# A row softmax: another split of the first loads, and a wait ahead of the third

## The chip, the cores and the metric

The kernel runs on one core of a Trainium2 chip. The metric is the device time of one execution in microseconds. Profile times count from the first instruction of the profiled execution (the start of its span). VectorE, ScalarE, GpSimd and SyncE stand in the profile as DVE, ACT, POOL and SP; a "q" behind an engine's name marks work of its instruction queue, such as the issue of a DMA. TensorE has no work here.

## The reference

The input x is float32 of 16 x 1024 x 512. Softmax is taken over the last axis:

```python
x_max = np.max(x, axis=-1, keepdims=True)
exp_x = np.exp(x - x_max)
return exp_x / np.sum(exp_x, axis=-1, keepdims=True)
```

That makes 16,384 rows of 512 elements (2 KB each). 33.55 MB are read and 33.55 MB are written.

## The kernel before

The 16,384 rows lie on 128 partitions, 128 rows to each. `CHUNKS` (line 13) cuts these 128 into ten chunks: the first number is the rows per partition, the second the place in the tile `held`, which has room for 96 rows per partition. The chunks have 3, 5, 8 and then seven times 16 rows. One load brings a chunk, all its rows of a partition as one contiguous piece: 6, 10, 16 or 32 KB per partition. In the text, load 1 is that of the first chunk, load 2 that of the second, and so on to load 10 (in the code they have the indices 0 to 9).

All work is in place in `held`. A chunk is worked on in groups of about 8 rows (`GROUP`; a chunk of 16 rows makes two groups). For each group there are three steps:

- `rowmax` (line 98): one VectorE reduction over the whole group, at line 101, which gives the negated maxima.
- `exps` (line 105): for each row one ScalarE exponential with the maximum as bias, which also gives the row's sum (line 109).
- `scale` (line 118): one VectorE reciprocal (line 121) and for each row one VectorE multiplication (line 123); then the store of the finished rows is issued on ScalarE's queue (line 129).

The order is written out by hand (line 136 and after). SyncE issues the loads, all at line 96. Indices 0 to 7 (`EARLY`) are issued ahead of everything else, and `loads_at_the_head` (line 33) puts the very first before the barrier at the program's start. The loads with the indices 8 and 9 go into places that earlier chunks have left; they are issued after the chunks with the indices 2 and 3 (`AFTER_STORE`) and wait for the stores of those rows. Each engine works in program order. The group loop takes the maxima and exponentials of a group before the scaling of the group ahead of it, except at the start of chunks with the indices 1, 2 and 3 (`FINISH_BEFORE`), where the earlier group is finished first. Each DMA counts up a semaphore when it lands. There are eight of these, and they are used again, so that some loads wait for an earlier DMA before they are issued: the sixth waits for the first, the seventh for the second and the eighth for the fourth.

Chunks with the indices 3, 4 and 5 are stored in two halves (`STORE_ROWS`), the others whole. That makes 13 stores.

Of the kernel before, what the change touches and what calls it, by code (L numbers as in the profile page):

```python
# [1 line left out]

# [4 lines left out]

F32 = mybir.dt.float32
EXP = mybir.ActivationFunctionType.Exp
AX = mybir.AxisListType.X  # L10


CHUNKS = [
    (3, 0), (5, 3), (8, 8), (16, 16), (16, 32), (16, 48), (16, 64), (16, 80), (16, 0), (16, 16),
]
SBUF_ROWS = 96

EARLY = 8
AFTER_STORE = {2: [8], 3: [9]}

GROUP = 8

FINISH_BEFORE = (1, 2, 3)

STORE_ROWS = {3: 8, 4: 8, 5: 8}

ON_ACT = ()

AT_HEAD = {mybir.EngineType.SP: 1}

def loads_at_the_head(nc):

    main, body = nc.main_func.blocks[0], nc.main_func.blocks[1]
    for engine, count in AT_HEAD.items():
        loads = [
            i
            for i in body.instructions
            if i.engine == engine and type(i).__name__ == "InstDMACopy"  # L40
        ][:count]
        barrier = next(
            n
            for n, i in enumerate(main.instructions)
            if i.engine == engine and type(i).__name__ == "InstDrain"
        )
        for load in loads:
            body.instructions.remove(load)
        main.instructions[barrier:barrier] = loads


@with_exitstack
def kernel(
    ctx: ExitStack,
    tc: tile.TileContext,
    x: bass.AP,
    out: bass.AP,
):
    nc = tc.nc
    nc.at_finalize(loads_at_the_head)  # L60
    P = nc.NUM_PARTITIONS

    x_flat = x.flatten_outer_dims()
    out_flat = out.flatten_outer_dims()
    n, d = x_flat.shape
    assert n == P * sum(R for R, _ in CHUNKS)


    src, dst, at = [], [], 0
    for R, _ in CHUNKS:  # L70
        for flat, views in ((x_flat, src), (out_flat, dst)):
            part = flat[at : at + P * R, :]
            views.append(part.rearrange("(p r) d -> p r d", r=R))
        at += P * R

    data = ctx.enter_context(tc.tile_pool(name="data", bufs=1))
    stats = ctx.enter_context(tc.tile_pool(name="stats", bufs=4))
    held = data.tile([P, SBUF_ROWS, d], F32, name="held")
    place = [held[:, s : s + R, :] for R, s in CHUNKS]


    groups = []
    for k, (R, _) in enumerate(CHUNKS):
        m = max(1, round(R / GROUP))
        cuts = [R * i // m for i in range(m + 1)]
        since = 0
        for a, b in zip(cuts, cuts[1:]):
            ends = b == R or b - since >= STORE_ROWS.get(k, R)
            groups.append((k, a, b, since if ends else None))
            since = b if ends else since  # L90
    shift = [None] * len(groups)
    sums = [None] * len(groups)

    def load(k):
        queue = nc.scalar if k in ON_ACT else nc.sync
        queue.dma_start(out=place[k], in_=src[k])

    def rowmax(g):
        k, a, b, _ = groups[g]
        shift[g] = stats.tile([P, b - a], F32, name="shift", tag="shift")  # L100
        nc.vector.reduce_max(  # L101
            out=shift[g], in_=place[k][:, a:b, :], axis=AX, negate=True
        )

    def exps(g):
        k, a, b, _ = groups[g]
        sums[g] = stats.tile([P, b - a], F32, name="sums", tag="sums")
        for r in range(a, b):
            nc.scalar.activation(  # L109
                out=place[k][:, r, :],  # L110
                in_=place[k][:, r, :],
                func=EXP,
                bias=shift[g][:, r - a : r - a + 1],
                scale=1.0,
                accum_out=sums[g][:, r - a : r - a + 1],
            )

    def scale(g):
        k, a, b, since = groups[g]
        recip = stats.tile([P, b - a], F32, name="recip", tag="recip")  # L120
        nc.vector.reciprocal(out=recip, in_=sums[g])  # L121
        for r in range(a, b):
            nc.vector.tensor_scalar_mul(  # L123
                out=place[k][:, r, :],
                in0=place[k][:, r, :],
                scalar1=recip[:, r - a : r - a + 1],
            )
        if since is not None:
            nc.scalar.dma_start(
                out=dst[k][:, since:b, :], in_=place[k][:, since:b, :]  # L130
            )
        if b == CHUNKS[k][0]:
            for later in AFTER_STORE.get(k, ()):
                load(later)

    with tc.manual_schedule():
        for k in range(EARLY):
            load(k)
        waiting = None
        for g, (k, a, _, _) in enumerate(groups):  # L140
            if waiting is not None and a == 0 and k in FINISH_BEFORE:
                scale(waiting)
                waiting = None
            rowmax(g)
            exps(g)
            if waiting is not None:
                scale(waiting)
            waiting = g
        scale(waiting)


# [1 line left out]
_INS = ['x']  # L153
_OUTS = [((16, 1024, 512), 'float32')]


# [23 lines left out]
```

## Time and profile before

| what | us |
|---|---|
| median of four runs | 161.55 |
| lowest, highest | 161.53, 161.78 |
| the profiled execution | 161.78 |
| its span, first to last instruction | 160.0 |
| VectorE busy | 123.9 |
| ScalarE busy | 93.3 |
| first load, issue to landing | 4.4 |
| second load (5 rows), issue to landing | 7.8 |
| third load (8 rows), issue to landing | 12.3 |
| last store issued at | 144.77 |

The profiled execution is the slowest of the four. What its time has beyond the span, 1.78 us, lies before the first and after the last instruction.

The busy time of an engine is the sum over its instructions, without issues of DMAs and waits. DMA is the mean busy share of sixteen DMA engines. Queue q1 holds the loads, q10 the stores. The trace also records each packet: here a packet is one partition's piece of a load or a store, and each of the sixteen DMA engines carries eight pieces of every load, and then a 4-byte mark that counts up the semaphore. GB/s of a window counts the packets that start in it.

### The profile page before, as it was taken

To read this page: it belongs to the slowest core of one execution; us is meant where nothing else is said; L and a number is where in the kernel's file an instruction comes from. 1 tells how busy PE (TensorE), PEld (TensorE's weight loads), DVE (VectorE), ACT (ScalarE), POOL (GpSimd) and SP (SyncE) were. 2 spreads that over 40 slices of the span, in tenths; PEclk is the share of its full clock that TensorE was granted. 3 is DMA by queue.
4 is the path that set the end of the run, shared out by engine and by line. 5 is a ranking of instruction groups with operands and counts; after the bars stand their busy time and mean duration, and the time that the engine had idled before them with its cause. 6 is when DMAs were issued, how large, how long until landed. Compare 5 with 4: busy or idle time off the path is not lost.

```text
span 160.0 us, 521 instructions
## 1 busy us (share of the span) xinstructions
DVE 123.9 (77%) x162; ACT 93.3 (58%) x257; POOL 0.2 (0%) x4
## 2 busy tenths in 40 slices
DVE  0481870799699999999999999999999999661000
ACT  0718029208994959595867777685959595930000
POOL 0000000000000000000000000000000000000000
DMA  7999999999999999999999999999999999999993
GB/s 253 374 475 373 446 456 416 417 426 452 406 428 438 483 410 399 434 442 467 406 414 434 442 463 418 399 442 418 442 447 451 410 434 467 401 426 475 410 426 164
DMA packets 3315, 67.13 MB, mean 420 GB/s; under 512 B 368, under 2 KB 368, under 8 KB 624
## 3 DMA queue, kind: packets, MB, share of 16 engines
q1 hardware_dynamic: 1440, 33.56, 49.5%
q10 hardware_dynamic: 1872, 33.56, 48.8%
q14 instruction: 3, 0.02, 0.0%
HBM read 33.55 MB, written 33.55 MB: 419 GB/s over the span
## 4 chain that ended last, share of the span: by engine, by line
DVE 70%; ACT 14%; issue 3%; DMA 3%; DVEq 0%; ACTq 0%
DVE shift L101 38%; DVE held L123 30%; ACT held L109 14%; DMA held<-in_x_dram 3%; DVE recip L121 2%; DVEq L175 0%; ACTq L109 0%
## 5 line engine op out<-in xcount | busy, mean ns | idle before, releaser
L109 ACT ACTIVATE held<-held,shift 128x512 f32<-128x512 f32 x128 | 90.5, 709 | 43.4 <-DVE shift L101 33.3
L101 DVE TENSOR_REDUCE shift<-held 128x8 f32<-128x4096 f32 (+2 forms) x17 | 70.7, 4162 | 4.5 <-DMA held<-in_x_dram 4.5
L123 DVE TENSOR_SCALAR held<-held,recip 128x512 f32<-128x512 f32 x128 | 52.2, 482 | 0.6
L109 ACT ACTIVATION_READ_ACCUMULATOR held<-held,shift 128x1 f32 x128 | 23.9, 187 | 0.0
L121 DVE RECIPROCAL recip<-sums 128x8 f32<-128x8 f32 (+2 forms) x17 | 3.3, 194 | 15.8 <-ACT held L109 15.8
L109 ACT ACT_TABLE_LOAD x1 | 1.3, 1283 | 4.5 <-DMA held<-in_x_dram 4.5
L164 POOL MEMSET const-bfloat16-1.0<- 128x1 bf16 x1 | 0.1, 102 | 0.0
L164 POOL MEMSET const-uint8-127<- 128x1 uint8 x1 | 0.1, 102 | 0.0
L164 POOL MEMSET const-float32-1.0<- 128x1 f32 x1 | 0.1, 99 | 0.0
L164 POOL MEMSET const-float32-0.0<- 128x1 f32 x1 | 0.1, 98 | 0.2 <-issue 0.2
## 6 DMA issues: line engine op xcount, KB each, us to landing
held<-in_x_dram SPq DMA_DIRECT2D x7, 4096.0 KB, 43.0
out_dram<-held ACTq DMA_DIRECT2D x4, 4096.0 KB, 21.3
out_dram<-held ACTq DMA_DIRECT2D x7, 2048.0 KB, 35.7
held<-in_x_dram SPq DMA_DIRECT2D x1, 2048.0 KB, 12.3
held<-in_x_dram SPq DMA_DIRECT2D x1, 1280.0 KB, 7.8
out_dram<-held ACTq DMA_DIRECT2D x1, 1280.0 KB, 19.5
held<-in_x_dram SPq DMA_DIRECT2D x1, 768.0 KB, 4.4
out_dram<-held ACTq DMA_DIRECT2D x1, 768.0 KB, 15.4
```

The source lines that it names most:

```text
L101: nc.vector.reduce_max(out=shift[g], in_=place[k][:, a:b, :], axis=AX, negate=True)
L109: nc.scalar.activation(out=place[k][:, r, :], in_=place[k][:, r, :], func=EXP, bias=shift[g][:, r - a : r - a + 1], scale=1.0, accum_out=s ...
L121: nc.vector.reciprocal(out=recip, in_=sums[g])
L123: nc.vector.tensor_scalar_mul(out=place[k][:, r, :], in0=place[k][:, r, :], scalar1=recip[:, r - a : r - a + 1],)
L164: nc = _bacc.Bacc("TRN2", target_bir_lowering=False, num_devices=1)
```

## The change

Two things change. The second and third chunk change places in size: the first loads have 3, 8 and 5 rows per partition, and the places in `held` follow. And each load from the third on is made to depend on the first: it is issued once the first has landed.

```diff
 CHUNKS = [
-    (3, 0), (5, 3), (8, 8), (16, 16), (16, 32), (16, 48), (16, 64), (16, 80), (16, 0), (16, 16),
+    (3, 0), (8, 3), (5, 11), (16, 16), (16, 32), (16, 48), (16, 64), (16, 80), (16, 0), (16, 16),
 ]
...
+ONCE_LANDED = 2
...
+    queued = [None] * len(CHUNKS)
     shift = [None] * len(groups)
     sums = [None] * len(groups)
 
     def load(k):
         queue = nc.scalar if k in ON_ACT else nc.sync
-        queue.dma_start(out=place[k], in_=src[k])
+        queued[k] = queue.dma_start(out=place[k], in_=src[k])
+        if k >= ONCE_LANDED:
+            tc.add_manual_dep(
+                queued[k].ins,
+                queued[0].ins.name,
+                mybir.DependencyInfo(
+                    mybir.DependencyClass.Sync, mybir.DependencyReason.DATA
+                ),
+                reason="the first load gets the descriptor generator first",
+            )
```

The second load carries no such wait. `add_manual_dep` makes the instruction named first wait for the completion of the second.

## The prediction

> **What bounds the kernel now.** I read the page's slices and queues first, then DMA rates by stretch, then the timelines of SP and VectorE, and last the packet records of the trace. The page, parts 2 and 3 (40 slices of 4 us; queue q1 carries the loads, q10 the stores; the last column is a share of sixteen DMA engines' time):
>
> ```profile
> DMA  7999999999999999999999999999999999999993
> GB/s 253 374 475 373 446 456 416 417 426 452 406 428 438 483 410 399 434 442 467 406 414 434 442 463 418 399 442 418 442 447 451 410 434 467 401 426 475 410 426 164
> ...
> q1 hardware_dynamic: 1440, 33.56, 49.5%
> q10 hardware_dynamic: 1872, 33.56, 48.8%
> ```
>
> The transfers fill 98.3% of the DMA engines' time in the span, from the second slice on without a hole. VectorE is busy 77%, ScalarE 58%. The chain of waits names VectorE for 70%, but that chain ends with the issue of the last store at 144.77 us, and the span ends at 160.0 us: what lies between is DMA alone. So bytes at the DMA rate set the end, and only a DMA stretch below its rate can be won or lost. Where such stretches are, the windows tell (length; VectorE, ScalarE, GpSimd busy; clock; DMA share; GB/s):
>
> ```profile
> 1.00:2.00 1.00, 0.00 (x0) 0.00 (x0) 0.00 (x0) 1.00 0.95 227
> 2.00:8.00 6.00, 1.75 (x1) 3.04 (x6) 0.00 (x0) 1.00 0.99 380
> 8.00:16.00 8.00, 4.18 (x5) 3.71 (x11) 0.00 (x0) 1.00 1.02 424
> 16.00:112.00 96.00, 87.89 (x108) 63.52 (x178) 0.00 (x0) 1.00 1.00 432
> 112.00:144.00 32.00, 29.35 (x48) 23.00 (x64) 0.00 (x0) 1.00 1.01 435
> 144.77:160.00 15.23, 0.00 (x0) 0.00 (x0) 0.00 (x0) 1.00 0.84 361
> ```
>
> From 16 to 144 us the rate is (96 x 432 + 32 x 435) / 128 = 433 GB/s, loads and stores together or stores alone. Against that the start is short: 1 to 2 us by 206 KB or 0.48 us, 2 to 8 us by 6 x 53 = 318 KB or 0.73 us, 8 to 16 us by 72 KB or 0.17 us. Everything this change can win from the DMA is in these 1.4 us. The engines are "busy" there, too: a packet takes longer than its like does later.
>
> **The change, part by part.** The issues on SP in order (start, length):
>
> ```profile
> 0.00 0.36 SPq L96 DMA_DIRECT2D held<-in_x_dram  x1
> 0.77 0.33 SPq L96 DMA_DIRECT2D held<-in_x_dram  x1
> 1.15 1.17 SPq L96 DMA_DIRECT2D held<-in_x_dram  x2
> 2.36 0.45 SPq L96 DMA_DIRECT2D held<-in_x_dram  x1
> 4.45 0.33 SPq L96 DMA_DIRECT2D held<-in_x_dram  x1
> 8.58 0.33 SPq L96 DMA_DIRECT2D held<-in_x_dram  x1
> ```
>
> An issue takes 0.33 us, but the third, fourth and fifth took 0.42, 0.69 and 0.45: something behind SP is full between 1.1 and 2.8 us. The sixth load waits for the landing of the first already, the seventh for that of the second.
>
> *The wait.* Loads 3, 4 and 5 move from 1.15-2.81 us to just after the first landing (4.45 us now), load 6 follows them. Behind the waiting load 3 on SP stand only loads. Four issues at 0.33 to 0.69 us end by 5.8 to 7.2 us. Load 7 waits for load 2, which is now the bigger one; load 8 waited until 25.16 us before and may do so again: more than 4 MB are queued ahead of each. No compute waits: 8 rows of load 3 were used from 18.63 us, its 5 rows now later still.
>
> *The cover.* Until load 3's bytes come, the DMA engines live on loads 1 and 2: 768 + 2048 KB = 2.884 MB. Up to 4.45 us they moved 227 + 406 + 379 + 0.45 x 389 = 1187 KB (1-us windows), so 1.70 MB are left, 3.9 us at 433. The very first load needed 1.01 us from issue to first packet. The cover is 2.9 us over; with 5 rows in second place it would be (2.097 - 1.187) / 433 = 2.1 us less 1.0. If it were gone, every us without packets would be one us at the end. I cost the wait itself at nothing.
>
> *What goes.* In the packet records, fourteen of the sixteen engines begin load 1 at 1.01 to 1.23 us and two at 1.80 and 1.83. Three packets of load 2 take 1.08, 1.19 and 1.22 us where 0.385 is usual. Completion marks of load 1 spread from 3.19 to 4.08 us, of load 2 from 6.62 to 8.25 (the latest: 7.51, 7.57, 7.60, 8.10, 8.25), of load 3 from 11.77 to 13.11, and those of the last store still from 157.41 to 158.78: an engine that loses time at the start never gets it back, and the slowest ends the kernel. The three long packets fall behind the crowded issues, and with these gone from there I take them as gone. What the slowest engine gains: with the two latest marks taken away, load 2 would end at 7.60 (0.65 earlier), load 3 at 12.67 (0.44); with the four latest taken from the last store, it would end at 158.36 (0.42). From below: nothing, if the long packets have another cause. From above: all of the 0.73 us of 2 to 8 us, and 0.95 with half of the first 0.48. I take **0.45 us**, nearest to the two later marks, since these have already been through what comes after.
>
> *What is added at the new place.* Four issues run while load 2 flows. The nearest row is the single issue at 4.45 us: 5 to 8 us moved 379, 399 and 328 GB/s, short by 193 KB or 0.45 us. Against it stands the next one at 8.58 us, the same form: 9 to 11 us moved 393 and 426, short by 47 KB or 0.11 us. So a late issue costs between 0 and 0.45 us and four between 0 and 1.8. I take the four together at what that stretch shows already, that is, no more than before, because load 2's packets were all handed over by then and the 8.58 us row is the nearer to it in that respect.
>
> *Rows 8 and 5 exchanged.* Reductions, exponentials and scalings of the 16 rows are the same instructions, so their sum on the chain is the same. But VectorE now wants 8 rows after the first 3. It is ready at 9.91 us:
>
> ```profile
> 4.46 1.75 DVE L101 TENSOR_REDUCE shift<-held 128x3 f32<-128x1536 f32 x1 [4.46 <-DMA held<-in_x_dram]
> 8.71 1.28 DVE L123 TENSOR_SCALAR held<-held,recip 128x512 f32<-128x512 f32 x3
> 9.91 2.81 DVE L101 TENSOR_REDUCE shift<-held 128x5 f32<-128x2560 f32 x1
> ```
>
> 2.884 MB had been moved at 8.0 + (2884 - 2507) / 492 = 8.8 us. Loads landed 1.8 us after their byte count was reached (load 2: count at 6.8, landed at 8.56), so 8 rows would land at 10.5; with even engines (lag 1.2, 0.45 less) at 9.2. The chain slips by 0 to 0.6 us, and an earlier first landing is eaten up there. At the end the cover is: after 144.77 us 15.23 x 361 = 5.50 MB still move, the last store is 4.19 MB, so 1.31 MB or 3.0 us of another store lie before it; less 1.0 us from issue to first packet leaves 2.0 us. A slip of 0.6 costs nothing; beyond 2.0 each us costs one. Load 9 waits for the stores of the first 16 rows, issued at 53.09 us; load 8 was landing until 81.6, so 28 us cover that.
>
> **A rule against it.** The Trainium skill, DMA: Bandwidth & Descriptors, section Rules for kernel authors, says to issue a DMA early and wait late; section Queues, rings and completion order says an engine takes descriptors in ring order, so a later load can't pass the first. By these, holding loads back wins nothing, and the sum is the old time, 161.55. The row against is the uneven first load itself, 3.19 to 4.08 us, with nothing but other loads behind it. That the added issues are what made it uneven, no row here proves.
>
> **Sum.** The profiled execution took 161.78 us, 1.78 outside its span; it is the slowest of the four, 0.23 above the median of 161.55. 161.78 - 0.45 = 161.33, and on the median's scale 161.55 - 0.45 = **161.1 us**.
>
> **Rivals.** About 0.2% (0.32 us) is what a measurement of this kernel can tell from no change.
> - *Forecast, 0.46:* the slowest engine gains 0.35 to 0.95 us: 160.6 to 161.2.
> - *It doesn't do what it says, 0.31:* load 2 is still issued 0.77 us after load 1, and the late engines at 1.80 us and the slow packets of 5.2 to 6.4 us are as before, or the long packets merely come later: 161.5 (161.23 to 161.87). For it: two late starters alone keep load 2 at 7.6 and the end within 0.4 us of now. Against it: three long packets just behind the crowded issues.
> - *The burst strikes load 2, slower, 0.20:* issues of loads 3 to 6 slow the packets under way as 5 to 8 us suggest. Between no addition and 4 x 0.45 - 0.73 = +1.07, the middle: +0.54, 162.1, up to 162.6. It decides from a shortfall of 0.73 + 0.32 = 1.05 us or 455 KB between 2 and 10 us on. Against it: 8.58 us.
> - *Other slower ones, 0.03:* the cover at either end breaks.
>
> So faster 0.46, same 0.31, slower 0.23. The range leaves out the end of the slow rival: 160.6 to 162.2.
>
> **What would show it.** Right: packets of load 2 all near 0.611 us, 2 to 8 us above 400 GB/s, marks of the last store closer together than 1.37 us. Load 1 should land before 4.4, yet VectorE still start the 8 rows at 9.2 to 10.5 us. Right on the wait: four issues after the landing, DMA full around 8 us. Wrong: long packets or under 380 GB/s from 5 to 9 us, or a hole at 8 to 9 us, or a gap in the stores after 144 us.

## The result and the profile after

The changed kernel takes 161.91 us (median of 35 runs), the kernel before 161.63 (56 runs); the ratio is 1.0022, interval 1.0011 to 1.0032. It is slower by 0.2%, and a gain of 0.45 us was forecast. In both kernels some executions take 0.5 to 1 us more than the rest, which shifts medians of few runs, so below the lower quartile (the time a quarter of the way up the sorted times) stands beside the median: 161.56 before, 161.82 after, 0.26 us apart. The lowest times are 161.46 and 161.67.

The profiled execution of the changed kernel took 161.76 us with a span of 160.0, as much as that of the kernel before. The page, part 2:

```profile
DMA  8999899999999999999999999999999999999993
GB/s 307 397 451 410 380 461 407 414 426 422 443 429 442 425 426 420 459 426 430 430 438 414 451 418 438 440 406 430 430 442 467 426 418 451 426 434 434 442 410 164
```

The same full line of nines: bytes at the DMA rate are the bound here too. The windows (columns as before):

```profile
1.00:2.00 1.00, 0.00 (x0) 0.00 (x0) 0.00 (x0) 1.00 0.82 313
2.00:8.00 6.00, 1.75 (x1) 3.16 (x6) 0.00 (x0) 1.00 1.03 417
8.00:16.00 8.00, 5.78 (x5) 2.12 (x7) 0.00 (x0) 1.00 1.06 430
16.00:112.00 96.00, 86.41 (x109) 64.99 (x182) 0.00 (x0) 1.00 1.00 428
112.00:144.00 32.00, 29.36 (x48) 23.00 (x64) 0.00 (x0) 1.00 1.01 437
```

At a glance this is the forecast come true, 380 GB/s risen to 417 between 2 and 8 us. And yet the end of this execution didn't move, because 16 to 112 us fell from 432 to 428. The issues on SP are where they were expected, four in a row from 4.33 us on:

```profile
0.78 0.33 SPq L99 DMA_DIRECT2D held<-in_x_dram  x1
4.33 0.33 SPq L99 DMA_DIRECT2D held<-in_x_dram  x1
4.71 0.43 SPq L99 DMA_DIRECT2D held<-in_x_dram  x1
5.18 0.45 SPq L99 DMA_DIRECT2D held<-in_x_dram  x1
5.67 0.49 SPq L99 DMA_DIRECT2D held<-in_x_dram  x1
```

VectorE starts the 8 rows at 9.79 us, no slip:

```profile
4.34 1.75 DVE L113 TENSOR_REDUCE shift<-held 128x3 f32<-128x1536 f32 x1 [4.34 <-DMA held<-in_x_dram]
8.59 1.28 DVE L135 TENSOR_SCALAR held<-held,recip 128x512 f32<-128x512 f32 x3
9.79 4.41 DVE L113 TENSOR_REDUCE shift<-held 128x8 f32<-128x4096 f32 x1
```

**Where the lead went.** From the packet records I take the bytes that have moved at a given time (a packet's bytes spread evenly over its duration) and divide the difference of two kernels by 433 GB/s. That is the lead in us over the first profile of the kernel before. For the changed kernel it is 0.65 at 8 us, 0.48 at 20, 0.41 at 24, 0.24 at 28, 0.13 at 34 and 0.05 to 0.06 from there to the end. The loss falls around the second store. The timeline of ScalarE's queue, changed kernel:

```profile
9.90 0.37 ACTq L141 DMA_DIRECT2D out_dram<-held  x1
23.54 0.34 ACTq L141 DMA_DIRECT2D out_dram<-held  x1
32.27 0.34 ACTq L141 DMA_DIRECT2D out_dram<-held  x1
```

With 8 rows in second place the second store is issued at 23.54 us; before it was 18.75 (with 5 rows), and the third store was about where it is now:

```profile
18.75 0.34 ACTq L129 DMA_DIRECT2D out_dram<-held  x1
32.39 0.34 ACTq L129 DMA_DIRECT2D out_dram<-held  x1
```

The first store is done on the DMA engines at 24.40 to 25.45 us, and the first packet of the second comes at 27.10. The queues between 25.5 and 27 us, the kernel before:

```profile
q1 hardware_dynamic: 16, 0.52, 80.9%
q10 hardware_dynamic: 16, 0.16, 25.7%
```

and the changed kernel, where the line of q10, the stores, is missing:

```profile
DMA packets 16, 0.52 MB, mean 350 GB/s; under 512 B 0, under 2 KB 0, under 8 KB 0
...
q1 hardware_dynamic: 16, 0.52, 91.8%
```

The loads are alone. Their 32 KB packets, 1.213 us otherwise, take up to 0.31 us more from 25.6 to 27 us.

### The profile page after: what moved, and what is told of

The parts are those of the page before. It is cut to its first block, busy times and chain, and to the rows that moved or that the text cites. A ratio compares the mean times of both kernels' runs of the same rounds, so it can differ in the third digit from the quotient of the medians.

```text
span 160.0 us, 516 instructions
## 1 busy us (share of the span) xinstructions
DVE 123.9 (77%) x162; ACT 93.3 (58%) x257; POOL 0.2 (0%) x4
## 4 chain that ended last, share of the span: by engine, by line
DVE 73%; ACT 14%; DMA 3%; issue 1%; DVEq 0%; ACTq 0%
DVE shift L113 41%; DVE held L135 30%; ACT held L121 14%; DMA held<-in_x_dram 3%; DVE recip L133 1%; DVEq L187 0%; ACTq L121 0%
```

## The experiments

Theory A, after the first comparison: the wait wins half a microsecond at the start, and the exchanged sizes lose it again through the late second store. Rival B: the held loads cost something later. Rival D came up with the first four runs: the starts differ by chance. In all experiments times are against the kernel before on the same chip.

**1. The wait alone.**

```diff
-    (3, 0), (8, 3), (5, 11), (16, 16),
+    (3, 0), (5, 3), (8, 8), (16, 16),
```

(against the changed kernel)

> The wait alone: sizes 3, 5, 8 as before, loads from the third on still held until the first has landed. Theory A (the start is faster by some 0.5 us, and the changed kernel gives it back between 24 and 36 us because its 8-row second chunk is stored at 23.5 instead of 18.8 us, so that the store queue runs empty when the first store ends at about 25 us and the loads alone go slower): the second store is issued near 18.7 us, the store queue has no hole at 25 us, 1 to 16 us stays as quick as in the changed kernel, and the end comes 0.3 to 0.6 us before that of the kernel before (161.0 to 161.3). Rival B (the held loads and their burst themselves cost something later, with the DMA engines closer in step): the lead is lost between 20 and 36 us here too, 161.6 to 161.9. Rival C (5 rows are too little cover): a hole in the loads at 6 to 8 us.

Measured: 162.38 us against 162.05, ratio 1.0019 (0.9992 to 1.0045); lower quartiles 162.28 and 161.59. Theory A's gain is not there, and rival C is the reading that fits best. Windows of this kernel:

```profile
2.00:8.00 6.00, 1.75 (x1) 3.05 (x6) 0.00 (x0) 1.00 0.96 363
6.00:7.00 1.00, 0.20 (x1) 0.77 (x3) 0.00 (x0) 1.00 1.21 363
7.00:8.00 1.00, 0.00 (x0) 1.00 (x4) 0.00 (x0) 1.00 0.71 289
```

The third load is issued at 4.44 us; the first engines end load 2 at 6.29, and the first packets of load 3 come from 6.3 us on. The ten that begin by 7.0 us take 0.35 to 0.7 us longer than usual, together 0.34 us per engine. Between 2.1 and 12 us an engine stood idle 0.34 us in the mean, in the kernel before 0.18, in the changed kernel 0.02. But less than 0.1 us of it lies at 6 to 7 us, and most at 3 to 5 us, before any held load had been issued: the hole that rival C foresaw is small, and the loss lies in the longer packets. One profile can't show that the wait made them: from 5 to 8 us packets ran over their usual time by 0.47 us per engine here, by 0.40 in the first profile of the kernel before, and by 0.12 in its second (experiment 8) and 0.06 in experiment 9. That the uncovered wait costs time rests on the times. The store queue has no hole at 25 us, and nothing is lost from 20 to 112 us (lead -0.23, then -0.19). Part of the time lies elsewhere: one DMA engine ended at 159.99 in this profile, all others by 158.72.

**2. The sizes alone.**

```diff
-    (3, 0), (5, 3), (8, 8), (16, 16),
+    (3, 0), (8, 3), (5, 11), (16, 16),
```

(against the kernel before)

> The sizes alone: 3, 8, 5 without the wait. Theory A: the start is that of the kernel before (380 GB/s in 2 to 8 us), the store queue is empty around 25 to 27 us, 0.4 to 0.6 us are lost there, and the end is the slowest of all, 162.0 to 162.3. Rival B: no loss between 20 and 36 us without the wait, 161.5 to 161.7.

Measured: 162.06 against 162.05, ratio 1.0003 (0.9974 to 1.0033), a wide interval; lower quartiles 161.92 and 161.59. The second store was issued at 24.16 us, and the lead fell from 0.07 at 20 us to -0.23 at 34. The loss is there without the wait: this speaks against B.

**3. The changed kernel, with the 8 rows in two groups and two stores.**

```diff
-        m = max(1, round(R / GROUP))
+        m = 2 if k == 1 else max(1, round(R / GROUP))
...
-STORE_ROWS = {3: 8, 4: 8, 5: 8}
+STORE_ROWS = {1: 4, 3: 8, 4: 8, 5: 8}
```

> The changed kernel with its 8-row second chunk worked on in two groups of 4 rows and stored in two halves, so that the second store is issued at about 17 us. Theory A: the store queue doesn't run empty at 25 us, the lead of 0.5 us from the start is kept to the end, 161.1 to 161.4. Rival B: the loss between 20 and 36 us stays, 161.7 to 162.0. One store more costs next to nothing either way.

Measured: 162.18 against 162.05, ratio 1.0017 (0.9995 to 1.0039); lower quartiles 162.03 and 161.59. The first half held: second store at 17.15 us, lead 0.53 at 20 us and 0.48 at 34. But from 90 to 100 us it lost 0.9 us, which nobody expected. The tenth load waits for the fourth chunk's second store, which landed at 90.79 (issue of the load: 90.87; 85.03 in the changed kernel), after the ninth load had landed at 90.18. The load queue was empty, and the packets with which it began again took up to 0.9 us more. One store more, in pieces of 8 KB, made the stores later (the store that was waited for was issued at 50.11 us; in experiment 6 the same store, issued at 49.99, landed at 82.64): each engine takes pieces of the two queues in turn (in the kernel before, the 5-row store beside loads took 12.8 us from the first mark of the store ahead to its own first, 8 times 1.213 for a load's piece and 0.385 for the store's), so that small pieces are a small share.

**4. A store held back, in the kernel before.** The store of the second chunk is issued right ahead of that of the third.

```diff
-            nc.scalar.dma_start(
-                out=dst[k][:, since:b, :], in_=place[k][:, since:b, :]
-            )
+            held_back.append((k, since, b))
+            if k != 1:
+                for kk, lo, hi in held_back:
+                    nc.scalar.dma_start(
+                        out=dst[kk][:, lo:hi, :], in_=place[kk][:, lo:hi, :]
+                    )
+                held_back.clear()
```

> The kernel before, with the store of its 5-row second chunk held back and issued together with that of the third (at 32.4 instead of 18.8 us). The output is the same. Theory A: the store queue is empty from about 25 to 35 us, loads alone run below 433 GB/s for these 8 to 10 us, and the loss is several times that of the changed kernel: 1 to 2 us, 162.5 to 163.5. Rival B: an empty store queue costs nothing while loads are queued, 161.5 to 161.7.

Measured: 162.16 against 162.05, ratio 1.0002 (0.9979 to 1.0025); lower quartiles 161.99 and 161.59. The store left at 24.52 us, not at 32.4, so this was a hole of 3 us only; the lead fell from 0.52 at 20 us to 0.25 at 34 and 0.15 at 42. The loss of the expectation, 1 to 2 us, was not tested. The lower quartile is 0.40 us above the kernel before and the lowest time 0.14 (161.65 and 161.51), with the sizes unchanged; the interval alone doesn't tell this from nothing. What this run did show: its start is the kernel before's, instruction for instruction, and yet it was 0.61 us ahead of that at 8 us, at 424 GB/s from 2 to 8 us. Thus rival D.

**5. The store held longer**, by issuing it after that of the third chunk:

```diff
-                for kk, lo, hi in held_back:
+                for kk, lo, hi in reversed(held_back):
```

> The kernel before, with the store of the 5-row second chunk issued after that of the third, so that no store is issued between 10 and 32 us (in the attempt before this one the held store still left at 24.5 us, since ScalarE's queue issues ahead of its exponentials). The output is the same. The store queue should be empty from about 25 to 35 us, four times as long as in the changed kernel. Theory A1 (loads alone are slower for as long as they are alone): a loss of 1 us or more between 24 and 40 us. Theory A2 (what costs is that the store queue begins again beside running loads, once): about 0.3 to 0.4 us, as in the changed kernel. Rival B: nothing.

Measured: 162.58 against 161.62, ratio 1.0058 (1.0038 to 1.0079). No store packet moves from 25.3 to about 36 us. The queues from 26 to 34 us, the kernel with the longer hold:

```profile
DMA packets 117, 3.31 MB, mean 414 GB/s; under 512 B 16, under 2 KB 16, under 8 KB 16
...
q1 hardware_dynamic: 117, 3.31, 96.0%
```

The packet count of that window is coarse; by the bytes the lead was 0.39 at 24 us and 0.44 at 34, while loads were alone, and -0.17 at 42. So A1 falls: loads alone keep the rate. The loss of 0.6 us came when the stores began again: load packets from 35.0 to 35.7 us took up to 0.8 us more. A2's mechanism stands, with a larger price than in the changed kernel. A second loss of 0.34 us came between 90 and 112 us: the tenth load was issued at 91.44, after the ninth had landed at 90.51, so that the load queue was empty as in experiment 3.

**6 and 7. Two groups of 4 rows, but one store**, with the wait and without.

```diff
-        m = max(1, round(R / GROUP))
+        m = 2 if k == 1 else max(1, round(R / GROUP))
```

> The changed kernel with its 8-row second chunk worked on in two groups of 4 rows but stored as one, so that its store is issued at about 20 us, before the first store has ended at 25; as many stores as before and of the same sizes as in the changed kernel. Theory A: no hole in the store queue, no loss between 24 and 38 us, the end 0.3 to 0.5 us before that of the changed kernel (161.3 to 161.5). Rival B: the loss stays.

> The same two groups with sizes 3, 8, 5 but without the wait. If the wait quickens the start, this is 0.3 to 0.6 us slower than the kernel with the wait and the two groups; if the difference between the starts is chance, both are alike, 161.4 to 161.7.

Measured: 161.69 with the wait, ratio 0.9997 (0.9977 to 1.0016), and 161.69 without, ratio 0.9998 (0.9982 to 1.0013), against 161.62; lower quartiles 161.59, 161.62 and 161.56. The store was issued at 19.86 and 20.04 us and its packets follow the first store's without a hole. With the wait:

```profile
19.86 0.34 ACTq L141 DMA_DIRECT2D out_dram<-held  x1
```

Both take the time of the kernel before: 0.2 us of what the exchange cost is won back by the earlier store, and the wait makes no difference. Two groups move every later store as well (the last to 140.99 and 141.18 us, from 144.65), so these runs don't single out the second. And the profiles don't fit theory A as it stood. The lead still fell from 0.45 to 0.10 and from 0.62 to 0.17 between 20 and 34 us; in the first, load packets that begin at 24.4 to 25.5 us, where each engine goes over from the first store to the second, take up to 0.58 us more. The hole isn't needed for that loss.

**8. The kernel before, profiled again.**

> The kernel before, profiled a second time, for how much its start differs from execution to execution. If its slow start is its own (theory A), the second load's completion marks again spread over 1.3 us or more with the last after 8.0 us, and 2 to 8 us run at 375 to 390 GB/s. If it is chance (rival D), the start may be as quick as in the changed kernel, 415 GB/s or so, and the gain of the wait in the changed kernel's profile is not shown.

Measured: 161.47 us, span 159.7. Its windows:

```profile
1.00:2.00 1.00, 0.00 (x0) 0.00 (x0) 0.00 (x0) 1.00 0.88 233
2.00:8.00 6.00, 1.75 (x1) 3.01 (x6) 0.00 (x0) 1.00 1.04 420
8.00:16.00 8.00, 4.18 (x5) 3.71 (x11) 0.00 (x0) 1.00 1.05 439
```

420 GB/s from 2 to 8 us, where the first profile had 380: the same program. The start does differ by chance, as rival D has it. The marks of the second load end at 7.74 us, at 8.25 in the first profile.

**9. The wait from the fourth load on**, sizes 3, 5, 8.

```diff
-ONCE_LANDED = 2
+ONCE_LANDED = 3
```

(with the sizes of the kernel before)

> Sizes 3, 5, 8 as before, and only the fourth and later loads wait for the first landing: the wait with 13 rows more behind the first load to cover it, without the change of sizes and so without the late second store. If the wait quickens the start (theory A), 161.0 to 161.3. If the starts differ by chance and the wait costs nothing once it is covered (theory D), the same as the kernel before, 161.5 to 161.7, with no idle DMA engine at 6 to 8 us.

Measured: 161.75 against 161.65, ratio 1.0014 (0.9993 to 1.0035); lower quartiles 161.60 and 161.56. No gain. The start is as quick as that of experiment 8:

```profile
2.00:8.00 6.00, 1.75 (x1) 3.09 (x6) 0.00 (x0) 1.00 1.02 423
```

**10 and 11. The changed kernel and the sizes alone once more, on one chip.**

> The changed kernel once more, on one chip with the other two: 0.2 to 0.35 us above the kernel before (161.8 to 161.9). Its start may be quicker or slower than in its first profile; theory D has a second profile with the lead at 20 us anywhere within 0.6 us, and the loss between 24 and 40 us again at 0.3 us or more.

> Sizes 3, 8, 5 without the wait, once more, beside the changed kernel. Theory D (all of the change's cost lies with the sizes, through the second store that comes late): the same as the changed kernel within 0.1 us, 161.8 to 161.9. If the wait itself costs something, this is 161.6 or below; if the wait helps, 162.0 or above.

Measured: 161.83, ratio 1.0009 (0.9993 to 1.0025), and 161.90, ratio 1.0013 (0.9996 to 1.0029), against 161.65; lower quartiles 161.78, 161.84 and 161.56. With and without the wait the same within 0.1 us, and both above the kernel before, though within each run's interval of it. The lowest times, 161.72 and 161.76 against 161.48, say the same as the lower quartiles.

All profiles side by side (lead in us over the first profile; "covered" is with 8 rows or more between the first load and the held ones; the lower quartile of the kernel before was 161.56 to 161.59 on the three chips):

| kernel | wait | second chunk's store, issue | lead at 20 us | 24 | 34 | 42 | lower quartile |
|---|---|---|---|---|---|---|---|
| before | no | 5 rows, 18.75 | 0 | 0 | 0 | 0 | 161.56 |
| before again (8) | no | 5 rows, 18.77 | 0.40 | 0.37 | 0.37 | 0.25 | (one run) |
| 9 | covered | 5 rows, 18.70 | 0.51 | 0.50 | 0.41 | 0.26 | 161.60 |
| 1 | not covered | 5 rows, 18.73 | -0.23 | -0.24 | -0.21 | -0.20 | 162.28 |
| 4 | no | 5 rows, 24.52 | 0.52 | 0.45 | 0.25 | 0.15 | 161.99 |
| 5 | no | 5 rows, 32.71 | 0.40 | 0.39 | 0.44 | -0.17 | 162.53 |
| changed | covered | 8 rows, 23.54 | 0.48 | 0.41 | 0.13 | 0.06 | 161.82 |
| changed again (10) | covered | 8 rows, 23.72 | 0.35 | 0.34 | 0.07 | 0.07 | 161.78 |
| 2 | no | 8 rows, 24.16 | 0.07 | 0.03 | -0.23 | -0.22 | 161.92 |
| 11 | no | 8 rows, 23.59 | 0.27 | 0.25 | 0.00 | 0.00 | 161.84 |
| 6 | covered | 8 rows, 19.86 | 0.45 | 0.41 | 0.10 | 0.09 | 161.59 |
| 7 | no | 8 rows, 20.04 | 0.62 | 0.53 | 0.17 | 0.16 | 161.62 |
| 3 | covered | 4 rows, 17.15 | 0.53 | 0.47 | 0.48 | 0.40 | 162.03 |

The lead counts the bytes of all sixteen engines, and the time follows the slowest one: in all thirteen profiles the execution took 2.9 to 3.1 us more than the last mark of the last store. In run 7 fifteen engines were done by 158.53 us, one at 159.01, and its execution took 162.01 us in spite of the lead.

## Why the prediction was wrong, point by point

- **What bounds the kernel** was right: DMA bytes, with VectorE's chain covered at both ends. As far as the runs show, VectorE and ScalarE touched the end in one way alone, through the time at which the second store was issued.
- **The step that failed** is "What goes": "The three long packets fall behind the crowded issues, and with these gone from there I take them as gone." Counting the packets of load 2 that take over 0.4 us more than usual, there are 3, 3, 1, 3, 3, 3 and 0 in seven profiles without the wait, and 1, 3, 0, 1, 2 and 2 in six with it. All of these begin between 3.15 and 4.39 us, among the first third of load 2's packets, and in the kernel before at 3.62, 4.21 and 4.21 us, 0.8 us and more after the crowded issues had ended at 2.81. Where the wait holds all loads from the third on, only loads 1 and 2 had been issued by then, and still they are there: neither the crowd nor its later burst makes them. The first load lands at 4.31 to 4.56 us without the wait and at 4.32 to 4.49 with it: the wait does not bring it sooner. And what I took for a property of the kernel, 380 GB/s from 2 to 8 us, is one draw: without the wait seven profiles have 380, 420, 424, 420, 389, 408 and 432, five with a covered wait 417, 413, 424, 417 and 423. A small gain in the mean (0.46 against 0.33 us of lead at 20 us) is not excluded by so few; in time there is none to be seen: the term of 0.45 us comes out at -0.04 in experiment 9 (lower quartiles), and at 0.06 and 0.03 between the pairs 10 and 11, 6 and 7.
- **The signs** that the prediction set for being right were no test. The changed kernel shows over 400 GB/s, load 1 landed at 4.32 us, and marks of the last store 1.25 us apart. But the kernel before, profiled again, has 420 GB/s and marks 1.16 us apart, and load 1 lands at 4.31 us in experiment 2, without the wait.
- **The cost of the exchanged sizes** was set at nothing, and that is where the slowdown comes from. I followed the chain on VectorE and the stores that free places, but not the store queue: the second store, later by 4.8 us, passes the end of the first. All six profiles with a whole 8-row second store lose 0.25 to 0.36 us between 24 and 34 us; the four with 5 rows stored at 18.7 us lose nothing to 0.09. Followed to 42 us the two kinds come near each other, 0.25 to 0.37 against nothing to 0.24, so the profiles alone don't carry this point; the times do. The sizes without the wait cost 0.28 and 0.33 us (lower quartiles of runs 11 and 2), as much as the whole change, and the lowest times with an 8-row store at 23.5 to 24.2 us are 161.67 to 161.83, against 161.46 for the kernel before and 161.54 to 161.56 for runs 6, 7 and 9. That it is the lateness of the store fits runs 4 and 5, where only the 5-row store was held: 0.40 us at 24.52 (lower quartiles; not beyond the interval), and 0.96 at 32.71 (medians; beyond it), some of this by the tenth load. Runs 6 and 7, with that store 3.7 us sooner, take the time of the kernel before, but there every later store is sooner, too.
- **The cover** was right in its logic and wrong in its size. I had 1.0 us from issue to first packet, the first load's row; in experiment 1 the first ten packets of load 3 began 1.9 to 2.6 us after its issue. The 2.1 us that 5 rows give by the prediction's own sum were thus too few on some engines, and the time bears it out: 0.69 us in lower quartiles with 5 rows behind the first load, 0.04 with 13 (experiment 9).
- **The burst** of four issues cost nothing: 417 GB/s from 2 to 8 us, no idle engine. The rival with that price is out, and so the slower side came by another way than any rival named. That 161.91 lies inside 160.6 to 162.2 is luck: the range reached so high for this rival alone.
- **The rule against the change**, to issue a DMA early and wait late, from the Trainium skill, DMA: Bandwidth & Descriptors, section Rules for kernel authors, agrees with these runs: covered, the held loads win nothing (161.75 against 161.65 us, experiment 9); uncovered, they lose (162.38 against 162.05, experiment 1). That a later load can't pass the first is the prediction's conclusion from the order in which an engine takes its descriptors; in all thirteen profiles the last mark of load 1 (4.22 us at the latest) comes before the first of load 2 (6.25 at the earliest).

What stays open: why the start differs by 0.6 us from execution to execution, and why the second store, with 8 rows whole, stretches load packets at 24 to 26 us even where the store queue has no hole (6 and 7), while the third store of the kernel before, 8 rows too, costs nothing in its first profile and 0.12 us from 34 to 42 us in its second. In 6 and 7 the loss stands in the profile and the time is nevertheless that of the kernel before; their starts in these two profiles were good ones, and at 42 us their leads, 0.09 and 0.16, lie among those of the kernel before, 0 and 0.25. One profile each cannot tell more. Dividing the second store without making the stores later as a whole wasn't tried.

## What to carry to other kernels

One profile of the kernel before is one draw of its start: before you explain a shortfall of half a microsecond, profile the same program twice. When DMA is the bound, a reordering has to be followed through every queue it feeds, stores as well as loads, to where a queue goes over to its next transfer, or runs empty and begins again. A wait that holds loads back needs cover for the whole delay from issue to first packet beside running traffic, here up to 2.6 us against 1.01 on an idle queue. And signs of success have to be such that the kernel before doesn't show them by chance.

## What the runs showed of the hardware that was not expected

- A store that is issued while loads are queued moved its first packet 3.6 to 3.8 us later: issue 23.54 and first packet 27.10 us in the changed kernel, 24.52 and 28.22 in experiment 4, 10.03 and 13.79 in the kernel before. The very first load, with nothing ahead of it, took 1.01 us.
- Where a queue began again beside a running one, the other's packets or its own took longer in these runs: load packets up to 0.8 us longer at 35 us in experiment 5, up to 0.9 at 95 to 98 us in experiment 3, for a loss of 0.6 and 0.9 us. Running empty is no condition of it: in experiment 6 load packets took up to 0.58 us more where one store followed another.
- ScalarE's queue issues ahead of its engine. In experiment 4 the store follows eight exponentials of the third chunk in the program; it was issued while the third of them ran, and the last ended at 28.6 us:

```profile
24.40 0.71 ACT L110 ACTIVATE held<-held,shift 128x512 f32<-128x512 f32 x1
24.52 0.34 ACTq L133 DMA_DIRECT2D out_dram<-held  x1
```
